# The second score product of 64-row heads over 128 rows, with zeros beside the keys' lower parts

## The chip, the cores and the metric

The kernel runs on one core of one Trainium2 chip. The metric is the device time of one execution in microseconds; smaller is better.

## What is computed

One batch of 512 tokens of width 1024 goes through two blocks. The first is a feed-forward layer, a mixer (retention and differential attention side by side), a cross-attention to a memory of 256 tokens and a second feed-forward layer. The second block is a neighbourhood attention, a gated embedding, a latent attention (MLA) and a second gated embedding. All is in float32. Three of the attentions have heads of 64 values; their scores are what the change is about:

```
retention       inner = einsum('bhnd,bhmd->bhnm', q, k) * decay          # 4 heads, d = 64
differential    s = einsum('bqhcd,bkhcd->bhcqk', q, k) * scale           # 4 heads x 2, d = 64
neighbourhood   s = einsum('bwhd,biwjhd->bhwij', q, k) * scale           # 16 heads, d = 64
```

The latent attention has heads of 96 values and is not touched; the cross-attention is not touched either.

## The kernel before

TensorE works on float32 operands that are split into an upper part (rounded to what TensorE takes) and a lower part (the rest). An ordinary product is three products, upper x upper, lower x upper and upper x lower (`mm3`, lines 265 to 267), accumulated in one PSUM tile. A split is a copy on ScalarE (upper part) and a subtraction on VectorE (lower part).

Weights come in pieces of 128 x 1024 through the SyncE queue, are split by ScalarE (L231) and VectorE (L232) and are held in three buffers. A projection tile is 8 steps of k with 3 products of 512 columns each.

**Scores of 64-row heads.** Two heads lie on top of each other in one 128-row tile. `stacked` (L462) makes the operands. For the operand that stands still in TensorE (`st`), one tile for each head holds the head's upper part in its own 64 rows and its lower part in the other 64. For the operand that moves (`mv`), one tile for each head holds the upper part twice (the second copy by a DMA, `move`, L1755), and a third tile, `x[2]`, holds the lower parts of both heads, each in its own 64 rows. `mm_stacked` (L490) then makes the scores with two products:

```
mm(out, st[hh][:, cs], mv[hh][:, cm], start=True, stop=False)      # L494: (upper; lower) x (upper; upper), 128 rows
mm(out, st[hh][r, cs], mv[2][r, cm], start=False, stop=True)       # L495: upper x lower, the head's 64 rows
```

It is called by `ret_s` (L800: 4 heads x 4 key tiles, 512, 384, 256 and 256 columns), by `dif_s` (L866: 4 heads x 4 query blocks, two calls behind each other in each, 256, 256, 384 and 512 columns) and by `s` of the neighbourhood attention (L1351: 16 heads x 4 query blocks, 256 columns): 16 + 32 + 64 = 112 pairs of products.

**Order.** TensorE and SyncE run in the order in which the program emits. The emission follows a clock of TensorE's work that the builder adds up (`pe`), and what the other engines do is put into a queue of events with delays. Between the scores, the transposes and the products with the values of an attention step, `fill` emits projection products ("filler"), in amounts given by the table `FILL`; the steps lie `LAG` apart (transposes two steps after the scores, products with values three or four). So while an attention waits for its softmax, TensorE has other work.

The set of operand tiles `y` (8 pairs `yh`, `yl` of 128 x 512) holds the feed-forward layer's hidden tiles, then the outputs of an attention's heads, and is read by the projection that follows. Head outputs are split into it at the end of a head (`ys`).

The row factors of a norm come by a chain (`rstd_chain`): TensorE transposes sums (L291), VectorE reduces (L304, L306), GpSimd takes a power (L311, tile `rs`), and TensorE transposes again (L317).

Of the kernel before, what the change touches and what calls it, by code (L numbers as in the profile page):

```python
# [11 lines left out]
F32R = mybir.dt.float32r  # L12
# [27 lines left out]
class Pr:  # L40
    """Whether the instructions that make something are emitted."""
# [6 lines left out]
class Act:  # L48
    """The two parts of an operand of a product."""
# [5 lines left out]
class Rows:  # L55
    """Factors of the rows of something: rs by partition, rb along the free axis."""
# [6 lines left out]
class Norm(Rows):  # L63
    """Operands x * gain, without the row factors, which come when all of x has been added."""
# [11 lines left out]
    def add(self, x, k, delay, later=0.0):  # L76
        """x, the k-th tile, is there delay us from now; its squares are not wanted until later us after that."""
# [28 lines left out]
class Builder:  # L106
    """Emits the program. Every engine runs its instructions as they are emitted; the emission follows a
    clock of the tensor engine, and what other engines do is emitted when its operands should be there."""
# [19 lines left out]
    # ------------------------------------------------------------- order of emission  # L128
# [3 lines left out]
    def ev(self, delay, fn, pr=None):  # L132
        """fn is emitted delay us from now."""
        pr = pr or Pr()
        self.seq += 1
        heapq.heappush(self.heap, (self.now() + delay, self.seq, fn, pr))
        return pr
# [12 lines left out]
    def when(self, pr, fn):  # L150
        """fn, which frees a product's place, is emitted as soon as pr is."""
        if pr.done:
            self.ev(0.1, fn)
        else:
            pr.then.append(fn)
            self.parked += 1
            self.parked_on = pr
# [20 lines left out]
    def fill(self, us):  # L178
        """Emits filler products worth us, as far as there are any."""
# [5 lines left out]
    # ------------------------------------------------------------- tiles  # L185
# [8 lines left out]
    def act(self, which, k):  # L194
        """The k-th tile pair of one of the two sets of operands."""
# [4 lines left out]
    # ------------------------------------------------------------- weights  # L200
# [17 lines left out]
    def halved(i, n):  # L218
        """The first pieces of all come in two halves, so that the arithmetic can begin."""
# [16 lines left out]
    def wget(self, pieces):  # L236
        """pieces: [(name, first row, columns)], 128 rows each, side by side."""
# [24 lines left out]
    # ------------------------------------------------------------- products  # L262
# [18 lines left out]
    # ------------------------------------------------------------- norms  # L281
    def rstd_chain(self, acc, nt, d, out, pr, slack, more=None):
        """From now on: sums over the partitions of acc [128, nt*128] give out.rs [128 tok, nt] and out.rb [128, nt*128]."""
# [51 lines left out]
    # ------------------------------------------------------------- parts that several phases have  # L335
    def gemm_list(self, items, acts, nk=KT, late=0):
        """items: [(pieces, evac(psum))], one product of 512 columns each. The first two take their last
        operands late."""
# [26 lines left out]
    def gate(self, cond):  # L365
        """Filler that has to wait for the attention to get on."""
# [8 lines left out]
    def proj(self, name, ys, xt, nxt, k0=0, nk=KT, scale=None, early=0, late=1):  # L375
        """x += y @ W (times scale); feeds the sums and operands of the next norm. The last early tiles have
        got the first half of it before."""
# [19 lines left out]
    def pairs(self, name, ms, acts, k0, nk, item):  # L397
        """Products of few k, two to a piece of weights."""
# [9 lines left out]
    def proj_early(self, name, ys, xt, early):  # L408
        """x += the first half of y @ W for the last early tiles."""
# [7 lines left out]
    def vproj(self, name, cols, acts, ntok, dst, nk=KT, w=None):  # L417
        """Rows of tokens of 256 columns: dst(i, psum) for every tile of tokens."""
# [22 lines left out]
    def split(self, hi, lo, src, delay=0.1, scale=None, pr=None, n=512):  # L441
        """hi and lo of src (times scale), which is there delay from now."""
# [19 lines left out]
    def stacked(self, mp, t, tag, moving, delay, pr):  # L462
        """Parts of t, two heads of 64 rows that are there delay from now, for products over 64 rows in two steps:
        upper and lower part on top of each other times the upper part twice, upper times lower part. Gives
        [first head, second head] or, of the operand that moves, [first head, second head, lower parts]."""
        nc = self.nc
        x = [mp.tile([P, 512], F32R, tag=f"{tag}{i}", name=self.nm(tag), bufs=2) for i in range(3 if moving else 2)]
# [9 lines left out]
        def second():  # L477
            a, b = (x[2][lo, :], x[2][hi, :]) if moving else (x[0][hi, :], x[1][lo, :])
# [10 lines left out]

    def mm_stacked(self, out, st, mv, hh, cs, cm):  # L490
        """out = product of columns cs of st and cm of mv over the rows of a head."""
        mm = self.nc.tensor.matmul
        r = slice(64 * hh, 64 * hh + 64)
        mm(out, st[hh][:, cs], mv[hh][:, cm], start=True, stop=False)  # L494
        mm(out, st[hh][r, cs], mv[2][r, cm], start=False, stop=True)  # L495
        self.pe(2 * out.shape[-1] / 2400)

    def softmax(self, sp, bias=None, to=None):
        """Rows of sp (psum [128 q, n]), plus bias if any, to probabilities in sbuf; returns (tile, Pr)."""
# [33 lines left out]
    def transposed(self, pt, hi, lo, n):  # L533
        """pt (psum) to hi and lo, as parts."""
        return self.split(hi, lo, pt, 0.1, n=n)

    def halves(self, t, hh, po, pr):
        """t[rows of head hh] = upper + lower half of po."""
# [13 lines left out]
    def gated(self, o, z, y, *prs):  # L552
        """y = o * z as parts, once prs are there."""
# [6 lines left out]
    def silu(self, z, ps, n, pr):  # L560
        """z = silu(ps times the row factors of n) from now on, as h + h tanh h with h half of the argument."""
# [13 lines left out]
    # ------------------------------------------------------------- phases  # L575
# [40 lines left out]
    def mix(self, n, xt, nxt):  # L616
        nc, tc = self.nc, self.tc
        with tc.tile_pool(name="mixp", bufs=1) as mp:
# [35 lines left out]
            for y in ys:  # L654
                y.pr = Pr()
# [1368 lines left out]
```

## Time and profile before

| | |
|---|---|
| median of 3 runs | 1880.83 us (1880.43 to 1881.2) |
| span of the profiled execution | 1879.1 us; its own time is not listed apart, and the median is 1.7 us above this span |
| TensorE busy (products) | 1846.8 us, 98% |
| TensorE weight loads | 1529.3 us, 81% |
| VectorE / ScalarE / GpSimd busy | 59% / 43% / 17% |
| mean DMA rate | 96 GB/s |
| retention | 397.7 to 489.9 us |
| differential attention | 489.9 to 586.5 us (its last scores), its tail to about 605 us |
| neighbourhood attention | 1190 to 1437 us (its last scores), its tail to about 1450 us |

Products are pipelined: the duration of one is longer than the distance to the next, and its end is modelled. What a product costs is read from start to start. Weight loads have rows of their own (PEld) and run beside the product before.

### The profile page before, as it was taken

What the parts mean: (1) busy time and instruction counts of PE and PEld (TensorE: products, weight loads), DVE (VectorE), ACT (ScalarE), POOL (GpSimd) and SP (SyncE); (2) the same over time, 40 slices, a digit from 0 to 9 for tenths busy, and PEclk for the clock granted to TensorE, in tenths of its full rate; (3) what the DMA queues carried; (4) which work ended last, traced back from release to release, by engine and by line L of the source; (5) the groups of instructions that cost most, each with busy time, mean ns of one, the idle gap of its engine ahead of it and who ended that gap; (6) DMA issues with size and microseconds to landing.
All of it is one profiled execution on the core that took longest, in us unless ns stands there. A gap on an engine that the chain in (4) does not pass through costs nothing.

```text
span 1879.1 us, 24338 instructions
## 1 busy us (share of the span) xinstructions
PE 1846.8 (98%) x9176; PEld 1529.3 (81%) x9176; DVE 1103.2 (59%) x1806; ACT 813.9 (43%) x1416; POOL 327.2 (17%) x317
## 2 busy tenths in 40 slices
PE   9999999999999999999999998999999999999997
PEld 7888888888876898888888886788888887888886
DVE  6434444556776755544344445666666667888646
ACT  5222222433554544432232234555554544666644
POOL 2000000310112211200000004322222221444322
PEclk9999999999999999999999999999999999999998
DMA  4222222422221332222323222323232223434222
GB/s 159 98 93 101 91 101 97 142 69 84 80 79 56 112 135 77 92 91 89 110 91 103 98 87 97 115 88 115 88 104 70 95 95 88 110 91 110 86 90 79
DMA packets 55556, 181.13 MB, mean 96 GB/s; under 512 B 7104, under 2 KB 9792, under 8 KB 55440
## 3 DMA queue, kind: packets, MB, share of 16 engines
q1 hardware_dynamic: 52480, 168.45, 27.3%
q0 software_dynamic: 2816, 11.08, 1.8%
q8 instruction: 73, 1.20, 0.3%
q14 instruction: 43, 0.35, 0.1%
q10 hardware_dynamic: 144, 0.05, 0.0%
HBM read 163.04 MB, written 2.10 MB: 88 GB/s over the span
## 4 chain that ended last, share of the span: by engine, by line
PE 92%; DVE 3%; ACT 2%; POOL 1%; issue 1%; DMA 1%; POOLq 0%; SPq 0%; DVEq 0%; ACTq 0%
PE mm L265 24%; PE mm L266 24%; PE mm L267 24%; PE mm L434 2%; PE mm L435 2%; PE mm L436 2%; PE sc L495 2%; PE av L1712 1%; PE tp L1690 1%; PE av L1394 1%; PE sc L494 1%; PE tp L1378 1%; PE sc L265 1%; PE sc L266 1%; PE sc L267 1%
## 5 line engine op out<-in xcount | busy, mean ns | idle before, releaser
L231 ACT ACTIVATE whi<-raw 128x1024 fp32r<-128x1024 f32 (+3 forms) x302 | 304.5, 1013 | 623.9 <-PE mm L266 429.5
L265 PE MATMUL mm<-xh,whi 128*128 128x512 f32 x1152 | 461.9, 401 | 3.5 <-ACT xh L450 3.5
L266 PE MATMUL mm<-xl,whi 128*128 128x512 f32 x1152 | 451.8, 392 | 5.7 <-DVE xl L457 5.6
L267 PE MATMUL mm<-xh,wlo 128*128 128x512 f32 x1152 | 451.3, 392 | 0.0
L232 DVE TENSOR_TENSOR wlo<-raw,whi 128x1024 fp32r<-128x1024 f32 (+3 forms) x302 | 363.7, 1207 | 64.5 <-ACT whi L231 61.1
L265 PE MATMUL mm<-yh,whi 128*128 128x512 f32 (+2 forms) x736 | 287.6, 391 | 2.3 <-ACT yh L448 2.3
L266 PE MATMUL mm<-yl,whi 128*128 128x512 f32 (+2 forms) x736 | 284.5, 387 | 0.5 <-DVE yl L455 0.5
L267 PE MATMUL mm<-yh,wlo 128*128 128x512 f32 (+2 forms) x736 | 284.2, 386 | 0.0
L265 PEld LDWEIGHTS mm<-xh,whi 128*128 128x128 f32 x1152 | 217.1, 188 | 55.5 <-ACT xh L450 5.2
L266 PEld LDWEIGHTS mm<-xl,whi 128*128 128x128 f32 x1152 | 217.5, 189 | 52.2 <-DVE xl L457 10.4
L267 PEld LDWEIGHTS mm<-xh,wlo 128*128 128x128 f32 x1152 | 217.1, 188 | 46.5 <-DVE wlo L232 0.3
L265 PEld LDWEIGHTS mm<-yh,whi 128*128 128x128 f32 (+1 forms) x736 | 138.1, 188 | 32.5 <-ACT yh L448 2.5
L267 PEld LDWEIGHTS mm<-yh,wlo 128*128 128x128 f32 (+1 forms) x736 | 138.2, 188 | 28.9
L266 PEld LDWEIGHTS mm<-yl,whi 128*128 128x128 f32 (+1 forms) x736 | 138.1, 188 | 28.3 <-DVE yl L455 1.1
L528 POOL TENSOR_TENSOR p<-p,st 128x512 f32<-128x512 f32 (+1 forms) x112 | 100.0, 895 | 249.5 <-DVE st L523 234.6
L99 POOL TENSOR_TENSOR acc<-acc,sq 128x512 f32<-128x512 f32 x54 | 92.7, 1718 | 166.9 <-ACT sq L95 166.5
L597 DVE TENSOR_TENSOR t<-mm,rb 128x512 f32<-128x512 f32 x44 | 30.4, 692 | 138.7 <-PE mm L267 138.7
L386 DVE SCALAR_TENSOR_TENSOR x<-mm,x 128x512 f32<-128x512 f32 x48 | 33.0, 691 | 119.9 <-PE mm L267 119.9
L588 DVE TENSOR_TENSOR t<-mm,rb 128x512 f32<-128x512 f32 x44 | 30.4, 692 | 94.2 <-PE mm L267 93.4
L434 PE MATMUL mm<-whi,xh 128*128 128x256 f32 x256 | 76.0, 297 | 0.0
L436 PE MATMUL mm<-whi,xl 128*128 128x256 f32 x256 | 72.4, 283 | 0.0
L435 PE MATMUL mm<-wlo,xh 128*128 128x256 f32 x256 | 72.4, 283 | 0.0
(315 smaller groups left out, 2807.2 us busy)
## 6 DMA issues: line engine op xcount, KB each, us to landing
raw<-in_wts SPq DMA_DIRECT2D x245, 512.0 KB, 3.5
raw<-in_wts SPq DMA_DIRECT2D x32, 448.0 KB, 3.3
bias<-in_nabias POOLq DMA_DIRECT2D x16, 384.0 KB, 3.4
kslot<-kt SPq DMA_DIRECT2D x16, 256.0 KB, 3.0
qs<-qt SPq DMA_DIRECT2D x16, 256.0 KB, 3.9
mv<-mv SPq DMA_DIRECT2D x28, 128.0 KB, 2.2
raw<-in_wts SPq DMA_DIRECT2D x12, 256.0 KB, 3.4
raw<-in_wts SPq DMA_DIRECT2D x8, 320.0 KB, 3.7
```

What stands on the lines that cost most here:

```text
L99: (nc.vector if k == KT - 1 else nc.gpsimd).tensor_tensor(self.acc, self.acc, t, OP.add)
L231: self.nc.scalar.activation(hi[:, c], raw[:, c], AF.Copy)
L232: pr = self.ev(0.3 + n / 1200, lambda c=c: self.nc.vector.tensor_tensor(lo[:, c], raw[:, c], b32(hi[:, c]), OP.subtract))
L265: mm(out, lh, rh, start=start, stop=False)
L266: mm(out, lh, rl, start=False, stop=False)
L267: mm(out, ll, rh, start=False, stop=stop)
L386: nc.vector.scalar_tensor_tensor(xt[m], ps, scale, xt[m], OP.mult, OP.add)
L434: mm(o, a.hi[:, t], w.hi[:, c], start=k == 0, stop=False)
L435: mm(o, a.hi[:, t], w.lo[:, c], start=False, stop=False)
L436: mm(o, a.lo[:, t], w.hi[:, c], start=False, stop=k == nk - 1)
L495: mm(out, st[hh][r, cs], mv[2][r, cm], start=False, stop=True)
L528: nc.gpsimd.tensor_tensor(p[:, :n], p[:, :n], st[:, 2:3].to_broadcast([P, n]), OP.mult)
```

## The change

The lower parts of the keys no longer share one tile. Each head gets a tile of its own for them, with the lower part in the head's own 64 rows and zeros in the other 64, and the second product runs over all 128 rows: the stationary tile's upper part meets the lower part, its lower part meets zeros. The zeros are written once at the start of the mixer and once at the start of the neighbourhood attention, into tiles 6 and 7 of the set `y`, which are free then; there are two pairs of such tiles, used in turn. The heads that write their outputs to tiles 6 and 7 take them when they are done. In the retention it is the queries that move, and the lower parts are theirs.

```diff
 def stacked(self, mp, t, tag, moving, delay, pr):
-    x = [mp.tile([P, 512], F32R, tag=f"{tag}{i}", name=self.nm(tag), bufs=2) for i in range(3 if moving else 2)]
+    x = [mp.tile([P, 512], F32R, tag=f"{tag}{i}", name=self.nm(tag), bufs=2) for i in range(2)]
+    if moving:
+        self.zi = 1 - self.zi
+        x.append(self.zl[self.zi])
...
     def second():
-        a, b = (x[2][lo, :], x[2][hi, :]) if moving else (x[0][hi, :], x[1][lo, :])
+        a, b = (x[2][0][lo, :], x[2][1][hi, :]) if moving else (x[0][hi, :], x[1][lo, :])
         nc.vector.tensor_tensor(a, t[lo, :], b32(x[0][lo, :]), OP.subtract)
         nc.vector.tensor_tensor(b, t[hi, :], b32(x[1][hi, :]), OP.subtract)
...
+def zeroed(self, tiles):
+    self.zi = 0
+    self.zl = [tiles[0:2], tiles[2:4]]
+    def zero():
+        for two in self.zl:
+            for c, t in enumerate(two):
+                self.nc.gpsimd.memset(b32(t[64 - 64 * c:128 - 64 * c, :]), 0.0)
+    self.zpr = self.ev(6.0, zero)
+
 def mm_stacked(self, out, st, mv, hh, cs, cm):
     mm = self.nc.tensor.matmul
-    r = slice(64 * hh, 64 * hh + 64)
+    self.need(self.zpr)
     mm(out, st[hh][:, cs], mv[hh][:, cm], start=True, stop=False)
-    mm(out, st[hh][r, cs], mv[2][r, cm], start=False, stop=True)
+    mm(out, st[hh][:, cs], mv[2][hh][:, cm], start=False, stop=True)
     self.pe(2 * out.shape[-1] / 2400)
...
 def mix(self, n, xt, nxt):
-    ys = [self.act("y", k) for k in range(KT)]
+    ys = [self.act("y", k) if k < 6 else Act(None, None) for k in range(KT)]
...
+    zs = [self.act("y", k) for k in (6, 7)]
...
     self.filler = prep()
+    self.zeroed([t for z in zs for t in (z.hi, z.lo)])
...
     # dif_av, done():
+    if h >= 2:
+        a = self.act("y", 4 + h)
+        ys[4 + h].hi, ys[4 + h].lo = a.hi, a.lo
     self.split(ys[4 + h].hi, ys[4 + h].lo, o, 0.75, pr=ys[4 + h].pr)
...
 def na(self, n, xt, nxt):
+    self.zeroed([t for z in [self.act("y", k) for k in (6, 7)] for t in (z.hi, z.lo)])
```

The order of instructions is the same before and after on TensorE, ScalarE and SyncE, but for the tile that the second product reads. TensorE, a score pair of the neighbourhood attention between a product with values (`av`) and filler (`mm`), before:

```order
L1394 MATMUL av_11360<-pt_9108,v_10446 128x256
L494 MATMUL sc_11369<-mv_11017,st_11072 128x256
L495 MATMUL sc_11369<-mv_11019,st_11072 128x256
L265 MATMUL mm_11315<-xh_9095,whi_11123 128x512
L266 MATMUL mm_11315<-xl_9096,whi_11123 128x512
```

and after the change:

```order
L1418 MATMUL av_11363<-pt_9110,v_10451 128x256
L510 MATMUL sc_11372<-mv_11021,st_11075 128x256
L511 MATMUL sc_11372<-yh_9115,st_11075 128x256
L265 MATMUL mm_11318<-xh_9097,whi_11126 128x512
L266 MATMUL mm_11318<-xl_9098,whi_11126 128x512
```

The second product of the pair now reads a `y` tile in place of the third `mv` tile; its neighbours are the same. (The list does not show that one has 64 rows and the other 128.)

GpSimd gets 8 memsets of 64 x 512. Four of them stand early in its queue, ahead of transfers and long idle time. The other four stand in two pairs, each between the last sum of squares of a norm (`acc`, L99) and the norm's power (`rs`, L311). The first of these places, at the end of the first feed-forward layer, before:

```order
L99 TENSOR_TENSOR acc_2348<-acc_2348,sq_2463 128x512
L99 TENSOR_TENSOR acc_2348<-acc_2348,sq_2499 128x512
L99 TENSOR_TENSOR acc_2348<-acc_2348,sq_2535 128x512
L311 TENSOR_TENSOR rs_2645<-rv_2639,small 128x4
L696 TENSOR_TENSOR t_2691<-t_2678,rcs 128x512
```

and after:

```order
L99 TENSOR_TENSOR acc_2348<-acc_2348,sq_2463 128x512
L99 TENSOR_TENSOR acc_2348<-acc_2348,sq_2499 128x512
L99 TENSOR_TENSOR acc_2348<-acc_2348,sq_2535 128x512
L502 MEMSET yl_2589 64x512
L502 MEMSET yh_2588 64x512
L311 TENSOR_TENSOR rs_2649<-rv_2639,small 128x4
L714 TENSOR_TENSOR t_2695<-t_2682,rcs 128x512
```

The two memsets wait for the last products that read tile 6 of `y`, and the power `rs` is queued behind them. The second such place is the same, at the end of the second feed-forward layer.

VectorE has one instruction elsewhere: at the end of the neighbourhood attention the lower part of head output 6 (`yl<-o,yh`) stands five places later. Its tile held zeros beside a lower part until the last score was made, so it waits for that product; the instruction right behind it (L527, the row maxima of that last score) waits for the same product.

## Rows read from the trace of the kernel before

**Rows 1.** The page's busy times and its chain of work that ended last, shares by engine.

```profile
PE 1846.8 (98%) x9176; PEld 1529.3 (81%) x9176; DVE 1103.2 (59%) x1806; ACT 813.9 (43%) x1416; POOL 327.2 (17%) x317
PE 92%; DVE 3%; ACT 2%; POOL 1%; issue 1%; DMA 1%; POOLq 0%; SPq 0%; DVEq 0%; ACTq 0%
```

**Rows 2.** Busy time of each engine in the stretches of the retention, the differential and the neighbourhood attention: length, PE, PEld, DVE, ACT, POOL busy (instructions), granted TensorE clock as a share of full speed, DMA share, GB/s.

```profile
397.70:489.90 92.20, 92.14 (x500) 75.65 (x499) 61.09 (x94) 37.17 (x61) 8.99 (x8) 1.00 0.24 81
489.90:586.50 96.60, 96.35 (x487) 75.11 (x486) 71.06 (x187) 50.24 (x112) 20.87 (x22) 1.00 0.22 73
1190.00:1437.00 247.00, 247.00 (x1368) 203.70 (x1367) 161.41 (x382) 135.71 (x295) 59.74 (x84) 1.00 0.29 98
```

**Rows 3.** The two products of a score pair over the whole program: minimum, median and maximum duration in ns, first and last start, forms.

```profile
L494 PE MATMUL sc<-mv,st x112: 276/282/503, 398.0 to 1436.2; 128*128 128x256 f32 x88, 128*128 128x512 f32 x12, 128*128 128x384 f32 x12
L495 PE MATMUL sc<-mv,st x112: 378/381/500, 398.3 to 1436.5; 64*128 64x256 f32 x88, 64*128 64x512 f32 x12, 64*128 64x384 f32 x12
```

**Rows 4.** TensorE in order of time around one score pair of the neighbourhood attention: start us, duration us, engine, line, operation, stationary rows * columns, moving operand.

```profile
1201.74 0.40 PE L267 MATMUL mm<-xh,wlo 128*128 128x512 f32 x1
1201.98 0.28 PE L494 MATMUL sc<-mv,st 128*128 128x256 f32 x1
1202.19 0.38 PE L495 MATMUL sc<-mv,st 64*128 64x256 f32 x1
1202.50 0.50 PE L265 MATMUL mm<-xh,whi 128*128 128x512 f32 x1
1202.83 0.40 PE L266 MATMUL mm<-xl,whi 128*128 128x512 f32 x1
```

**Rows 5.** TensorE at products over 128 rows behind each other, of 384 columns and of 512 and 256, in the retention.

```profile
483.27 0.34 PE L265 MATMUL av<-ah,vh 128*128 128x384 f32 x1
483.45 0.34 PE L266 MATMUL av<-al,vh 128*128 128x384 f32 x1
...
486.31 0.39 PE L267 MATMUL mm<-xh,wlo 128*128 128x512 f32 x1
486.54 0.28 PE L265 MATMUL av<-ah,vh 128*128 128x256 f32 x1
486.66 0.28 PE L266 MATMUL av<-al,vh 128*128 128x256 f32 x1
```

**Rows 6.** The weight loads around the score pair of rows 4, same columns.

```profile
1201.75 0.19 PEld L494 LDWEIGHTS sc<-mv,st 128*128 128x128 f32 x1
1202.19 0.18 PEld L495 LDWEIGHTS sc<-mv,st 64*128 64x128 f32 x1 [0.25 <-issue]
1202.49 0.19 PEld L265 LDWEIGHTS mm<-xh,whi 128*128 128x128 f32 x1
```

**Rows 7.** TensorE at a score pair of the retention with 512 columns, first row the first product of the pair, last row the second filler product behind it.

```profile
397.96 0.40 PE L494 MATMUL sc<-mv,st 128*128 128x512 f32 x1
...
399.04 0.40 PE L266 MATMUL mm<-xl,whi 128*128 128x512 f32 x1
```

**Rows 8.** TensorE at two score pairs behind each other in the differential attention, 384 columns: the first product of the first pair, and the second filler product behind the second pair.

```profile
501.72 0.34 PE L494 MATMUL sc<-mv,st 128*128 128x384 f32 x1
...
503.43 0.39 PE L266 MATMUL mm<-xl,whi 128*128 128x512 f32 x1
```

**Rows 9.** TensorE in the latent attention, a change from 128 to 96 rows.

```profile
1694.28 0.28 PE L1712 MATMUL av<-ptl,s 128*128 128x256 f32 x1
1694.39 0.40 PE L265 MATMUL sc<-kslot,qs 96*128 96x512 f32 x1
1694.62 0.40 PE L266 MATMUL sc<-kslot,qs 96*128 96x512 f32 x1
```

**Rows 10.** Neighbourhood attention: the row maxima of a score (VectorE), and the first product of the score two steps later, which writes the same PSUM buffer (TensorE).

```profile
1339.74 0.42 DVE L511 CUSTOM_DVE_ANT_0 pm<-sc,bias 128x256 f32<-128x256 f32 x1 [1.39 <-PE sc L495]
...
1342.85 0.28 PE L494 MATMUL sc<-mv,st 128*128 128x256 f32 x1
```

**Rows 11.** Differential attention: the power of a head's norm (GpSimd), and on TensorE two score pairs and the transposes that wait for the power.

```profile
570.36 1.01 POOL L311 TENSOR_TENSOR rs<-rv,small 128x4 f32<-128x4 f32 x1 [1.07 <-DVE rv L306]
...
569.42 0.36 PE L494 MATMUL sc<-mv,st 128*128 128x256 f32 x1
570.03 0.39 PE L494 MATMUL sc<-mv,st 128*128 128x256 f32 x1
572.14 0.38 PE L317 MATMUL tp<-ident,rs 128*128 128x128 f32 x2
```

**Rows 12.** The lower part of a head output on VectorE in the neighbourhood attention (busy us, mean ns of one), and TensorE's one wait at the end of the mixer.

```profile
L455 DVE TENSOR_TENSOR yl<-o,yh 128x512 fp32r<-128x512 f32 x7 | 5.3, 751 | 4.9 <-ACT yh L448 4.9
604.62 0.50 PE L265 MATMUL mm<-yh,whi 128*128 128x512 f32 x1 [2.26 <-ACT yh L448]
```

**Rows 13.** The two places of the new memsets on GpSimd: the power `rs` at each, the last TensorE product ahead of it that reads a tile of `y`, and the group of 128 x 512 sums on GpSimd (busy us, mean ns of one).

```profile
371.52 0.39 PE L267 MATMUL mm<-yh,wlo 128*128 128x512 f32 x1
1151.82 0.39 PE L267 MATMUL mm<-yh,wlo 128*128 128x512 f32 x1
378.12 1.04 POOL L311 TENSOR_TENSOR rs<-rv,small 128x4 f32<-128x4 f32 x1 [7.03 <-DVE rv L306]
1157.06 1.03 POOL L311 TENSOR_TENSOR rs<-rv,small 128x4 f32<-128x4 f32 x1 [6.34 <-DVE rv L306]
L99 POOL TENSOR_TENSOR acc<-acc,sq 128x512 f32<-128x512 f32 x54 | 92.7, 1718 | 166.9 <-ACT sq L95 166.5
```

## The prediction

> **What bounds the kernel now.** First the page: TensorE has products running in 98% of the span and makes up 92% of the chain that ended last [rows 1]. Then the busy times of the three stretches that the change touches: in the retention and the differential attention TensorE is idle for 0.06 and 0.25 us, in 247 us of the neighbourhood attention for none, and its clock is granted in full in all three [rows 2]. The other engines have room: VectorE, the next, is busy 66%, 74% and 65%. So a microsecond that TensorE no longer needs there should come off the time, unless another engine turns out late.
>
> But a busy TensorE is not one at its peak, since the durations overlap. The two products of a score pair write the same number of columns, and yet the one over 64 rows takes 381 ns and the one over 128 rows 282 ns at the median [rows 3]. What a pair costs is seen in the starts [rows 4]. The first product of the pair starts at 1201.98, the second, over 64 rows, 0.21 later, the next 0.31 later, and the one after that 0.33 later. Elsewhere, with 128 rows throughout, what follows a product of 512 columns starts 0.23 us behind it, 384 columns take 0.18 and 256 take 0.12 [rows 5]. The loads show why [rows 6]: the load of the first product runs beside the product before (1201.75 against a product start at 1201.74), but the load for 64 rows begins only at 1202.19, together with its own product, after 0.25 us in which the loader stood still, and the load that follows it again only at 1202.49. The loader cannot run ahead into or out of the 64-row product; the pipe of TensorE runs empty twice at each pair.
>
> **The change part by part.**
>
> *The pair itself.* Removed: 112 products over 64 rows. Added: 112 over 128 rows with the same columns. I take it that a 128-row product among 128-row products has the ordinary distance. From the start of the pair to the start of the second product behind it:
>
> - Neighbourhood attention, 256 columns: 1202.83 - 1201.98 = 0.85 us. Ordinary: 0.12 + 0.12 + 0.23 = 0.47. Saved 0.38. 64 pairs: 24.3 us.
> - Retention, 512 columns: 399.04 - 397.96 = 1.08 [rows 7], ordinary 3 x 0.23 = 0.69, saved 0.39; 16 pairs, the narrower ones taken alike: 6.2 us.
> - Differential attention, two pairs behind each other, 384 columns: 503.43 - 501.72 = 1.71 [rows 8], ordinary 4 x 0.18 + 0.23 = 0.95, saved 0.76 for two pairs; 16 such: 12.2 us.
>
> Together 42.7 us, 0.38 a pair. Bounds: if only the step into the 64-row product went (0.21 to 0.12) and what lies behind it stayed, 0.09 a pair, 10 us; reading errors of 0.02 us a pair upwards, 45 us. I take 42.7, since a product of 96 rows, which also fills less than the array, follows a 128-row product after 0.11 us and is followed after 0.23 [rows 9]: a product that leaves rows out does not by itself empty the pipe, one over 64 does. The Trainium skill, "TensorEngine Tiling (Array Packing)", Tiling Modes, Key Properties, says that a change of the tiling mode, not merely of the tile, drains TensorE, and it lists 64 rows as a mode and 96 not; the trace agrees, with two empty stretches a pair, and by that rule the whole 0.38 goes.
>
> *Freed time given back.* Steps get 0.38 us shorter (0.76 in the differential attention), while the chains of the other engines keep their length. In the neighbourhood attention the shortest reserve of a score's PSUM buffer is 1342.85 - (1339.74 + 0.42) = 2.69 us [rows 10]; two pairs within it take 0.77 away. Nothing is lost there. In the differential attention a head's norm has a power that ends at 571.37 and transposes that wait for it at 572.14: 0.77 us reserve, and the two pairs at 569.42 and 570.03 lie close to it [rows 11]. They are worth 0.76, so this wait comes to about zero, and a few others like it may cost some tenths. The wait of 2.26 us at the end of the mixer [rows 12] stays: its chain begins after the last scores, and the pairs before shift it as a whole. Given back: 0 to 3 us, I take 0.7.
>
> *The memsets.* Four of the eight stand ahead of transfers, where GpSimd has long been idle, and cost nothing. The other four stand in two places ahead of a norm's power. No memset of this size is in the trace; above, I take the sums of 128 x 512 on GpSimd, 1.72 us each [rows 13], below, nothing; nearest is the sum, for its engine and its 512 columns, and it is dear for a memset of half the rows. They may begin when the last product that reads the tile is done (371.52 + 0.39 = 371.9 and 1151.82 + 0.39 = 1152.2 [rows 13]) and end by 375.3 and 1155.6 at the latest; the powers start at 378.1 and 1157.1. They are hidden with 2.8 and 1.5 us to spare. If that cover were gone, each microsecond past it would stand on TensorE, which waits for the power's transposes.
>
> *Moved on VectorE, and the rest.* One subtraction of 0.75 us [rows 12] now stands ahead of the last score's row maxima and waits for the product that these wait for too; it delays them by 0.75 us, against a reserve of 2.69: nothing. The subtractions write two tiles in place of one, equally many and equally large; no transfer is added or moved on any queue.
>
> Sum: 42.7 - 0.7 = 42 us. The profiled execution has a span of 1879.1 us, which would become 1837; the median of the runs lies 1.7 us above that span, so 1880.8 becomes **1838.8 us**, 2.2% less.
>
> **The rivals.**
>
> *The time comes back as waits.* The fillers were laid out for steps of the old length, and VectorE's load in the differential attention rises from 74% to 71 / 84 = 84%. Against it: the reserves above, and that TensorE idles there for 0.3 us in all now [rows 2]. If a third of the gain came back, mostly in the differential attention and the norms: 14 us, 1853 us.
>
> *The gap belongs to the place, not to the 64 rows,* and the change does not do what it says. If the second load stood still because it reads the tile that the first has just loaded, or if a load ran ahead only into rows that are not in use, full rows would not help and the distances of 0.21, 0.31 and 0.33 would stay: 1880 us, no change; with only the step into the second product gone, 10 us, 1871 us. "TensorE: Matmul & The Clock Gate" of the Trainium skill, Part 3, What overlaps and what doesn't, says that weight loads overlap running products only when their row groups differ; by it full rows never overlap. The trace differs: the load at 1201.75 covers all 128 rows and starts beside a product over all 128 rows [rows 4, 6].
>
> *Slower, by the memsets.* GpSimd's power of a norm is queued behind two memsets at two places, and TensorE behind the power. Past the reserves of 2.8 and 1.5 us, each place costs its excess. To turn a gain of 42 us into a loss of over 3.8 us, the four memsets would need 46 + 4.3 + the 6.9 already allowed = 57 us, 14 us each, eight times the nearest row. If the pair's gain failed as well, 3.8 us of loss would need (3.8 + 4.3 + 6.9) / 4 = 3.8 us each, 1885 us. That is the point from which it decides.
>
> **How the numbers follow.** A measurement of this kernel can tell about 0.2%, 3.8 us, from no change. The forecast, 1833 to 1845: 0.79. The time given back, 1845 to 1862: 0.11. Only the step into the product, about 1871: 0.05. No change: 0.03, of it 0.01 for loads that run ahead only into unused rows. Slower: 0.02. The range has the first case whole and about half of the second: 1833 to 1851 us, some 0.85. Faster by over 0.2%: 0.95; within it 0.03; slower 0.02.
>
> **What would show it.** Right: the second product of a pair (L511 in the changed kernel) at about 282 ns, as the first; starts 0.12 us apart in a pair of 256 columns and 0.23 behind; loads of second products that begin beside the first; the neighbourhood attention shorter by about 24 us, the differential by 12 and the retention by 6, and everything outside unchanged. Given back: new waits of TensorE for `rs`, for row maxima or for split weights. Memsets: waits of L317 for `rs` at 379 and near 1140 us. The forecast is wrong if the loads of second products still begin with their own product, or if the three stretches shrink by less than 35 us together.

## The result and the profile after

The changed kernel takes 1840.38 us at the median (1839.84 to 1841.4, 4 runs) against 1880.98 us (1880.43 to 1881.2, 4 runs) for the kernel before: ratio 0.9785, 95% interval 0.9771 to 0.9799. The forecast was 1838.8 us in a range of 1833 to 1851. The span of the profiled execution falls from 1879.1 to 1838.2 us.

Where rows of the kernel after follow, they answer to rows shown of before, named by their groups. First the page, busy times and chain, beside [rows 1]:

```profile
PE 1803.2 (98%) x9176; PEld 1520.4 (83%) x9176; DVE 1098.7 (60%) x1806; ACT 810.9 (44%) x1416; POOL 330.1 (18%) x325
PE 91%; DVE 3%; ACT 2%; POOL 2%; issue 1%; DMA 0%; SPq 0%; POOLq 0%; DVEq 0%; ACTq 0%
```

TensorE still bounds the kernel. The number of its products is the same, and their busy time is 43.6 us less; the weight loads are busy 8.9 us less only. Most of what went from the span, 32.0 of 40.9 us, is time in which the loader stood still (349.8 us before, 317.8 after: span less busy time).

The two products of a pair over the whole program, beside [rows 3] (minimum, median, maximum in ns, first and last start; the second product reads `yh` for one head of a tile and `yl` for the other; the row shown is that of `yh`):

```profile
L510 PE MATMUL sc<-mv,st x112: 277/283/500, 398.4 to 1395.5; 128*128 128x256 f32 x88, 128*128 128x512 f32 x12, 128*128 128x384 f32 x12
L511 PE MATMUL sc<-yh,st x56: 274/283/400, 398.7 to 1386.6; 128*128 128x256 f32 x44, 128*128 128x512 f32 x6, 128*128 128x384 f32 x6
```

The second product has come from 381 to 283 ns, the first's own value. One pair of the neighbourhood attention in order of time, beside [rows 4], and its loads, beside [rows 6]:

```profile
1185.23 0.28 PE L510 MATMUL sc<-mv,st 128*128 128x256 f32 x1
1185.34 0.28 PE L511 MATMUL sc<-yh,st 128*128 128x256 f32 x1
1185.46 0.40 PE L265 MATMUL mm<-xh,whi 128*128 128x512 f32 x1
1185.70 0.40 PE L266 MATMUL mm<-xl,whi 128*128 128x512 f32 x1
...
1185.01 0.19 PEld L510 LDWEIGHTS sc<-mv,st 128*128 128x128 f32 x1
1185.23 0.19 PEld L511 LDWEIGHTS sc<-yh,st 128*128 128x128 f32 x1
1185.35 0.19 PEld L265 LDWEIGHTS mm<-xh,whi 128*128 128x128 f32 x1
```

The starts lie 0.11, 0.12 and 0.24 apart, 0.47 in all where it was 0.85. Each load begins with the product before it: the load of L511 at 1185.23, where L510 starts, and that of L265 at 1185.35, where L511 has just started. The 0.25 us of stillness ahead of the second load is gone.

The three stretches, cut at the same instructions as in [rows 2], with its columns:

```profile
398.16:484.04 85.88, 85.84 (x500) 75.26 (x499) 60.86 (x94) 37.25 (x61) 8.99 (x8) 1.00 0.27 87
484.04:570.10 86.06, 84.44 (x488) 73.30 (x488) 69.25 (x186) 48.58 (x112) 19.22 (x22) 1.00 0.26 79
1173.65:1395.90 222.25, 222.25 (x1368) 197.13 (x1367) 158.42 (x379) 133.38 (x293) 59.00 (x83) 1.00 0.33 109
```

The retention is 6.3 us shorter, the differential attention 10.5, the neighbourhood attention 24.75. Since TensorE's order did not change, every instruction of one trace can be set against the same one of the other: their difference is +0.46 us up to the retention (one wait at the start of the program came out longer), -5.9 behind it, -16.4 behind the differential attention, the same -16.4 until the neighbourhood attention begins, and -41.1 from its end to the end of the program. Outside the three stretches nothing moved.

Of the three stretches only the differential attention has TensorE idle more than before: 1.62 us where it was 0.25 (and two waits in its tail, behind the last scores, are 0.24 us longer each). The largest piece is one wait, at the transposes that [rows 11] show with a reserve of 0.77 us. In the trace after, TensorE reaches the transposes that feed this norm (L291) at 553.08; then VectorE, GpSimd and TensorE:

```profile
553.08 0.60 PE L291 MATMUL tp<-ident,t 128*128 128x128 f32 x4
554.18 0.68 DVE L304 TENSOR_REDUCE rv<-tp 128x4 f32<-128x512 f32 x1
555.51 0.75 DVE L929 SCALAR_TENSOR_TENSOR p<-p,dst,p 128x512 f32<-128x512 f32 x1 [0.65 <-POOL p L925]
556.17 0.16 DVE L306 TENSOR_SCALAR rv<-rv 128x4 f32<-128x4 f32 x1
556.48 1.01 POOL L311 TENSOR_TENSOR rs<-rv,small 128x4 f32<-128x4 f32 x1 [1.01 <-DVE rv L306]
557.54 0.65 PE L317 MATMUL tp<-ident,rs 128*128 128x128 f32 x4 [1.09 <-POOL rs L311]
```

and the same place before, TensorE's L291 and VectorE (L910 is what is now L929):

```profile
568.15 0.60 PE L291 MATMUL tp<-ident,t 128*128 128x128 f32 x4
568.79 0.69 DVE L304 TENSOR_REDUCE rv<-tp 128x4 f32<-128x512 f32 x1 [0.70 <-PE tp L291]
569.39 0.74 DVE L910 SCALAR_TENSOR_TENSOR p<-p,dst,p 128x512 f32<-128x512 f32 x1
570.05 0.16 DVE L306 TENSOR_SCALAR rv<-rv 128x4 f32<-128x4 f32 x1
```

From L291 to L306 it took 1.90 us before and takes 3.09 now. On VectorE a step of the softmax (L929) that waits for GpSimd stands ahead of L306, which starts only when that step is nearly done (556.17). TensorE comes to L291 15.07 us earlier than before, but that step comes only 13.88 us earlier, so the norm's chain grew by 1.19 us besides losing 0.76 us of cover. 1.19 + 0.76 - 0.77 = 1.18, and the wait is 1.09.

The memsets, in the first of the two places where something could have waited for them (GpSimd), beside [rows 13], and the transposes behind:

```profile
372.20 0.52 POOL L502 MEMSET yl<- 64x512 f32 x1 [0.66 <-PE mm L266]
372.78 0.52 POOL L502 MEMSET yh<- 64x512 f32 x1
378.64 1.04 POOL L311 TENSOR_TENSOR rs<-rv,small 128x4 f32<-128x4 f32 x1 [5.35 <-DVE rv L306]
...
380.18 0.60 PE L317 MATMUL tp<-ident,rs 128*128 128x128 f32 x4
```

A memset takes 0.52 us, where the nearest row gave 1.72. GpSimd then waits 5.35 us for its input, and L317 waits for nothing. The second place is the same (1135.69 to 1136.78, power at 1140.77 after 3.99 us of waiting; L317 waits 0.08 us there, where it was 0.01).

### The profile page after: what moved, and what is told of

It reads as the page before. It is cut to its first block, busy times and chain, and to the rows that moved or that the text cites. A ratio compares the mean times of both kernels' runs of the same rounds, so it can differ in the third digit from the quotient of the medians.

```text
span 1838.2 us, 24354 instructions
## 1 busy us (share of the span) xinstructions
PE 1803.2 (98%) x9176; PEld 1520.4 (83%) x9176; DVE 1098.7 (60%) x1806; ACT 810.9 (44%) x1416; POOL 330.1 (18%) x325
## 4 chain that ended last, share of the span: by engine, by line
PE 91%; DVE 3%; ACT 2%; POOL 2%; issue 1%; DMA 0%; SPq 0%; POOLq 0%; DVEq 0%; ACTq 0%
PE mm L266 24%; PE mm L265 24%; PE mm L267 24%; PE mm L434 2%; PE mm L435 2%; PE mm L436 2%; PE av L1736 1%; PE tp L1714 1%; PE av L1418 1%; PE tp L1402 1%; PE sc L265 1%; PE sc L266 1%; PE sc L267 1%; POOL acc L99 1%; PE sc L510 1%
## 5 line engine op out<-in xcount | busy, mean ns | idle before, releaser
L265 PE MATMUL mm<-xh,whi 128*128 128x512 f32 x1152 | 455.5, 395 | 3.9 <-ACT xh L450 3.9
L265 PE MATMUL mm<-yh,whi 128*128 128x512 f32 (+2 forms) x736 | 286.5, 389 | 2.3 <-ACT yh L448 2.3
L265 PEld LDWEIGHTS mm<-xh,whi 128*128 128x128 f32 x1152 | 217.4, 189 | 48.0 <-ACT xh L450 5.7
L265 PEld LDWEIGHTS mm<-yh,whi 128*128 128x128 f32 (+1 forms) x736 | 138.0, 188 | 30.8 <-ACT yh L448 2.5
L99 POOL TENSOR_TENSOR acc<-acc,sq 128x512 f32<-128x512 f32 x54 | 92.4, 1712 | 167.9 <-ACT sq L95 167.5
```

Source lines behind the costliest of these rows:

```text
L99: (nc.vector if k == KT - 1 else nc.gpsimd).tensor_tensor(self.acc, self.acc, t, OP.add)
L265: mm(out, lh, rh, start=start, stop=False)
```

## Experiments

The theory: an isolated product over 64 rows among products over 128 makes TensorE's loader stand still on entering and on leaving, 0.38 us in all, wherever it stands. The rivals: that the gap belongs to the place of the second product (the same stationary tile as the product before it, the accumulation); that any product with fewer than 128 rows has it; that memsets are dearer than they look; that the differential attention gives more back than its waits show.

**Grouping in place of padding** (on the kernel before). The order of a double pair of the differential attention becomes first, first, second, second, still with 64 rows in the second products:

```diff
+    w = max(nn, 256)
+    sps = [self.ps("sc") for _ in range(2)]
...
     for c in range(2):
-        sp = self.ps("sc")
-        w = max(nn, 256)
-        self.mm_stacked(sp[:, :w], qs, ks, c, t, slice(0, w))
+        mm(sps[c][:, :w], qs[c][:, t], ks[c][:, 0:w], start=True, stop=False)
+    for c in range(2):
+        r = slice(64 * c, 64 * c + 64)
+        mm(sps[c][:, :w], qs[c][r, t], ks[2][r, 0:w], start=False, stop=True)
...
```

> The kernel before, with the four products of a step of the differential attention in another order: both first products (128 rows), then both second products (64 rows each, the upper and the lower half of the rows). Theory (the pipe runs empty once on the way into and once on the way out of a stretch of 64-row products, 0.38 us a stretch): 16 stretches in place of 32, 16 x 0.38 = 6.1 us less, 1874.8 us; if the two 64-row products also run side by side, up to 16 x 0.12 us more, 1873. Rival 'place' (the second load stands still because it reads the stationary tile that the first one has just loaded): the first load of the other head now lies between, so both gaps would go, 32 x 0.2 to 32 x 0.38 = 6 to 12 us. Rival 'each product that leaves rows out pays': no change, 1880.8.

Measured: 1873.41 us (1872.75 to 1874.6, 5 runs) against 1880.76, ratio 0.9961 (0.9947 to 0.9974): 7.35 us gained. TensorE and its loads at one such group of 384 columns (x2: two instructions behind each other):

```profile
501.12 0.52 PE L882 MATMUL sc<-mv,st 128*128 128x384 f32 x2
501.57 0.44 PE L885 MATMUL sc<-mv,st 64*128 64x384 f32 x2
501.94 0.50 PE L265 MATMUL mm<-xh,whi 128*128 128x512 f32 x1
502.28 0.39 PE L266 MATMUL mm<-xl,whi 128*128 128x512 f32 x1
...
500.89 0.42 PEld L882 LDWEIGHTS sc<-mv,st 128*128 128x128 f32 x2
501.57 0.19 PEld L885 LDWEIGHTS sc<-mv,st 64*128 64x128 f32 x2 [0.26 <-issue]
501.94 0.19 PEld L265 LDWEIGHTS mm<-xh,whi 128*128 128x128 f32 x1 [0.18 <-issue]
```

From the first start to 502.28 it is 1.16 us, where [rows 8] have 1.71 and products over 128 rows throughout would have 0.95. The stillness of the loader stands once a group (0.26 us on the way in, 0.18 on the way out), not once a pair. The load that stands still follows the load of the other head's tile, so its cause is not that it reads the tile just loaded. The two loads over 64 rows take 0.19 us together, as one alone does, and the two products 0.44 us together, no longer than one of them: they start 3 ns apart, at every width. Upper and lower half of the rows work beside each other.

So the 0.55 us that a group saves has two parts: one way in and out less (0.38), and a second product that costs no distance of its own (0.18 at 384 columns). By the median starts of the three widths (256, 384, 512 columns) it is 8 x 0.50 + 4 x 0.56 + 4 x 0.60 = 8.6 us. Of these the trace gives back about 1.6 us in the same attention, 0.54 and 0.45 of it at the transposes that wait for `rs`; 7.35 was measured. The time alone does not tell the theory from the rival of the place, which had 6 to 12 us; the loads do.

**Both products over 64 rows** (on the kernel before, neighbourhood attention only; the lower parts of the queries are left out of the scores there, since the first product runs over the head's upper part alone):

```diff
-    mm(out, st[hh][:, cs], mv[hh][:, cm], start=True, stop=False)
+    q = r if self.half else slice(0, 128)
+    mm(out, st[hh][q, cs], mv[hh][q, cm], start=True, stop=False)
...
 def na(self, n, xt, nxt):
+    self.half = True
```

> The kernel before, with the first product of a score pair of the neighbourhood attention over the head's 64 rows too; it leaves out the product of the lower parts of the queries with the upper parts of the keys. Theory (each stretch of 64-row products pays once, on the way in and on the way out): a stretch is now two products long, no gap between them, the same price as before: 1880.8 us, within 2. Rival 'each product that leaves rows out pays' (0.38 each): 64 x 0.38 = 24 us more, 1905. Rival 'place' (the second load waits for the first one's tile): the gap of 0.21 between the two stays and nothing is added, 1880.8 too, but the starts then still lie 0.2 apart inside the pair, where the theory has 0.12.

Measured: 1880.53 us (1879.71 to 1881.55, 10 runs), ratio 0.9999 (0.999 to 1.0008). The pair and its two loads:

```profile
1201.59 0.40 PE L267 MATMUL mm<-xh,wlo 128*128 128x512 f32 x1
1201.91 0.38 PE L495 MATMUL sc<-mv,st 64*128 64x256 f32 x1
1202.14 0.28 PE L496 MATMUL sc<-mv,st 64*128 64x256 f32 x1
1202.35 0.50 PE L265 MATMUL mm<-xh,whi 128*128 128x512 f32 x1
1202.68 0.40 PE L266 MATMUL mm<-xl,whi 128*128 128x512 f32 x1
...
1201.91 0.18 PEld L495 LDWEIGHTS sc<-mv,st 64*128 64x128 f32 x1 [0.36 <-issue]
1202.02 0.19 PEld L496 LDWEIGHTS sc<-mv,st 64*128 64x128 f32 x1
```

From the product ahead of the pair to the second behind it: 1.09 us, and 1.09 before [rows 4]. One 64-row product or two, the price is one. Theory and rival of the place both had this time, and inside the pair the starts lie 0.23 apart (0.22 at the median of the 64 pairs): that is the rival's sign, not the theory's 0.12. The loads speak against the rival. The one that stands still is now the first product's (0.36 us), and the second product's load starts at 1202.02, ahead of its own product, though it reads the same tile as the first.

The starts suggest how the price is made up. What they have above the ordinary distance is 0.09, 0.19 and 0.10 around a single 64-row product [rows 4], and 0.09, 0.11, 0.09 and 0.10 here. So it looks as if the first product behind a change of rows comes 0.09 us late and the next another 0.10, on the way in as on the way out, and the 0.23 inside the pair would be the second of these. No run tests this by itself.

**64 rows elsewhere** (on the changed kernel; in the fourth k step of the gate and up products of the first and second feed-forward layer, 88 products, half the rows of the product with the weights' lower part are left out):

```diff
+    if self.cut and k == 3:
...
+        mm(out, w.hi[:, c], a.hi, start=False, stop=False)
+        mm(out, w.hi[:, c], a.lo, start=False, stop=False)
+        mm(out, w.lo[0:64, c], a.hi[0:64, :], start=False, stop=False)
...
```

> The changed kernel, with one product of the feed-forward layers' gate and up projections (the third of the fourth k, 88 in all, 512 columns) over 64 rows; the other 64 rows of that step are left out. No score, no stationary tile that is read twice running. Theory: 88 x 0.39 = 34 us more, 1875 us, with loads of those products that begin with their own product. Rival 'place' (the gap belongs to the score pair): no change, 1840.4.

Measured: 1874.35 us (1873.96 to 1875.61, 5 runs; ratio to the kernel before 0.9968, 0.9955 to 0.998), 34.0 us over the changed kernel: 0.386 us each. The group of these loads and products, with the loader's idle time ahead of them:

```profile
L278 PE MATMUL mm<-xh,wlo x88: 493/498/502, 12.2 to 1129.8; 64*128 64x512 f32 x88
its engine sat idle before it (us, times) until:
  issue: 31.3, 88
```

All 88 have it, 0.36 us of idle loader apiece. Here the stationary operand is not that of the product before, the accumulation goes on, and neighbours are ordinary weights: the gap belongs to the 64 rows.

**96 rows** (on the changed kernel). For the first head of each tile the second product leaves out the last 32 rows, which hold zeros:

```diff
-    mm(out, st[hh][:, cs], mv[2][hh][:, cm], start=False, stop=True)
+    r = slice(0, 96) if hh == 0 else slice(0, 128)
+    mm(out, st[hh][r, cs], mv[2][hh][r, cm], start=False, stop=True)
```

> The changed kernel, with the second product of the upper head of each pair of heads (56 of 112) over 96 rows, 32 rows of zeros, in place of 128. Theory in the form that 96 rows run in the same way of working as 128: no change, 1840.4. Rival 'each product that leaves rows out pays': 56 x 0.38 = 21 us more, 1862.

Measured: 1840.11 us (1839.62 to 1841.63, 4 runs; ratio 0.9785, 0.9772 to 0.9799), as the changed kernel. Products over 96 rows have 284 ns at the median, those over 128 rows 283. So leaving out 32 rows costs nothing, and leaving out 64 does; other counts were not tried.

**Second product left out** (on the changed kernel; upper x lower is missing in all 112 pairs):

```diff
-    mm(out, st[hh][:, cs], mv[hh][:, cm], start=True, stop=False)
-    mm(out, st[hh][:, cs], mv[2][hh][:, cm], start=False, stop=True)
+    mm(out, st[hh][:, cs], mv[hh][:, cm], start=True, stop=True)
```

> The changed kernel without the second product of a score pair (the upper parts of the queries times the lower parts of the keys are left out). Theory (TensorE still sets the pace of the score stages, and a second product costs its ordinary distance): 88 x 0.12 + 12 x 0.18 + 12 x 0.23 = 15.5 us less than 1840.4, 1825 us; a little is given back in the differential attention, so 1825 to 1827. Rival 'the other engines have become the bound of those stages': clearly less than 15 us, 1832 or more.

Measured: 1830.83 us (1829.56 to 1831.01, 4 runs; ratio 0.9731, 0.9718 to 0.9745), 9.6 us under the changed kernel where the starts promised 15.5, between theory and rival. By the same instruction in both traces: the neighbourhood attention gave 7.5 of 7.7, the retention 2.4 of 2.6, and the differential attention with its tail lost 0.4 where 5.2 had been expected; 0.9 was lost in the latent attention, where a wait for a transfer came up, and 0.45 came from the program's start. TensorE's waits in the differential attention:

```profile
529.64 0.65 PE L317 MATMUL tp<-ident,rs 128*128 128x128 f32 x4 [0.77 <-POOL rs L311]
553.24 1.12 PE L317 MATMUL tp<-ident,rs 128*128 128x128 f32 x4 [2.90 <-POOL rs L311]
572.86 0.63 PE L941 MATMUL tp<-ident,p 128*128 128x128 f32 x4 [1.35 <-DVE p L928]
```

The wait of 1.09 us has become 2.90 at the same transposes, and behind it TensorE ran at the lower clock for a while: granted 0.60 over the next 3.8 us (the column behind the engines' busy times), a mean of the level of 1.2 GHz and that of 2.4, while it stayed full behind the 1.09 us.

```profile
553.20:557.00 3.80, 3.76 (x15) 3.19 (x16) 2.32 (x6) 0.62 (x2) 0.40 (x1) 0.60 0.38 124
557.00:560.00 3.00, 3.00 (x19) 2.61 (x18) 2.43 (x8) 1.59 (x5) 0.00 (x0) 1.00 0.05 21
```

So the differential attention has no reserve left after the change: what TensorE saves there now comes back whole. The theory of the gap is not touched by it; the estimate was too large because it took the stretch for bound by TensorE.

**Ten memsets for each one** (on the changed kernel):

```diff
-    for c, t in enumerate(two):
+    for c, t in [x for x in enumerate(two) for _ in range(10)]:
```

> The changed kernel with each of the 8 memsets ten times. One takes 0.52 us in the changed kernel's trace and they follow at 0.58. Theory (they are hidden up to a point and then stand on TensorE, one for one): ahead of the first norm's power 20 of them, 11.5 us from 372.2, end at 383.7; the power began at 378.6, and its transposes had 0.5 us more: 4.6 us later. Ahead of the second power 12 of the 20 stand in the queue, 6.9 us from 1135.7, end at 1142.6; the power began at 1140.8: 1.8 us later, and 8 more memsets lie ahead of the sums of the next norm, 0 to 4.6 us. In all 6.4 to 11 us more than 1840.4: 1847 to 1851. Rival 'memsets on GpSimd stay hidden behind the products': no change.

Measured: 1847.69 us (1847.13 to 1847.83, 4 runs; ratio 0.9822, 0.9808 to 0.9835), 7.3 us more. The transposes behind the two places:

```profile
385.21 1.11 PE L317 MATMUL tp<-ident,rs 128*128 128x128 f32 x4 [4.47 <-POOL rs L311]
1150.32 0.65 PE L317 MATMUL tp<-ident,rs 128*128 128x128 f32 x4 [1.91 <-POOL rs L311]
```

Now they wait, 4.47 and 1.91 us, which shifts these two instructions by 4.63 and 1.84 us against the changed kernel's trace, as forecast. Behind the first wait another 1.4 us go, for the granted clock is 0.62 over the 4 us that follow, in part at the level of 1.2 GHz; behind the second, of 1.91 us, it stays full:

```profile
385.00:389.00 4.00, 3.79 (x13) 3.24 (x14) 0.00 (x0) 0.60 (x1) 0.15 (x1) 0.62 0.00 0
...
1150.00:1154.00 4.00, 3.68 (x18) 3.13 (x19) 2.88 (x3) 2.61 (x5) 3.67 (x8) 1.00 0.37 131
```

Behind the second place TensorE catches up 0.4 us at waits that it has there anyway. With 0.4 us of a longer start the span is 7.8 us longer, the median 7.3. The other two places lose nothing. The rival's mechanism is real and its path is as described (memset, power, transposes, TensorE); with one memset of 0.52 us in place of ten the power still waits for its input, and nothing is lost.

**More time for two norms** (on the changed kernel; the slack of the differential attention's norms shifts L317 behind more filler):

```diff
-    head_norm(PO.pop(h), done, SLACK["dif"])
+    head_norm(PO.pop(h), done, (0.48, (1.6, 2.2, 0.94, 0.94)[h]))
```

> The changed kernel, with the transposes that wait for a head norm's power in the differential attention emitted 0.7 us (first head) and 1.3 us (second head) later, so that more filler stands ahead of them. Theory (the gain lost in the differential attention is TensorE's waits of 0.5 and 1.1 us for these powers): 1.6 us less, 1838.8 us, and no wait for the power left there. Rival (the filler that fills the wait is missing elsewhere, or the outputs of the heads come late): no change, 1840.4.

Measured: 1841.96 us (1841.55 to 1843.52, 5 runs; ratio 0.9793, 0.978 to 0.9807). The forecast of 1838.8 us failed: the time is 1.6 us above the changed kernel's. The waits for `rs` in this stretch fell from 0.53 and 1.09 us to 0.23 us in all, and a wait at one of the last head's steps has taken their place:

```profile
576.27 1.09 PE L942 MATMUL tp<-ident,p 128*128 128x128 f32 x4 [2.99 <-DVE p L929]
...
576.20:580.00 3.80, 3.58 (x14) 3.03 (x15) 1.44 (x2) 1.53 (x3) 0.10 (x1) 0.50 0.00 0
```

Its 2.99 us, and the clock at 0.50 (1.2 GHz) in the 3.8 us behind it, cost more than the waits that went.

**More time for one norm** (as the last, for the second head alone):

```diff
-    head_norm(PO.pop(h), done, SLACK["dif"])
+    head_norm(PO.pop(h), done, (0.48, (0.94, 1.6, 0.94, 0.94)[h]))
```

> From the changed kernel: the norm of the second head of the differential attention alone gets more time (second delay 1.6 in place of 0.94), so that its transposes L317 stand behind one more group of three filler products of 512 columns (0.69 us by the starts); nothing else on TensorE moves, so the transposes and values of the later steps keep their places. Theory (the wait of 1.09 us for rs is the one loss that the shorter steps made in this head, and filler ahead of it covers it): the wait falls to about 0.4 us, TensorE is 0.6 to 0.7 us earlier from there on, and the time is 1839.7 us, which the trace can show and the times hardly. Rival (as with more time for two heads: the filler that is used here is missing a few steps later, and a wait for split weights p takes its place): 1840.4 us or more, with a new wait of L942.

Measured: 1841.26 us (1840.45 to 1841.87, 5 runs; ratio 0.9791, 0.9777 to 0.9804), not to be told from the changed kernel. TensorE's two waits, and VectorE's instruction ahead of the second:

```profile
557.60 0.65 PE L317 MATMUL tp<-ident,rs 128*128 128x128 f32 x4 [0.42 <-POOL rs L311]
574.30 0.55 PE L942 MATMUL tp<-ident,p 128*128 128x128 f32 x3 [2.02 <-DVE rv L304]
...
569.60 1.38 DVE L929 SCALAR_TENSOR_TENSOR p<-p,dst,p 128x384 f32<-128x384 f32 x1 [1.03 <-POOL p L925]
```

The first wait fell from 1.09 to 0.42, as the theory said, and TensorE ran 0.65 us earlier for the 16 us behind it; then its wait at the last steps of the last head grew from 0.80 to 2.02 us and took it all back. That place is paced by VectorE. The rival had the end right, a wait of L942, but not its cause: here no filler is missing, TensorE comes earlier and VectorE 0.55 later. So what was given back in this attention was not had by giving one or two of its norms more time; other places for the filler were not tried. No kernel here that computes everything is clearly faster than the changed one.

## Why the prediction was right

**The pair itself.** 42.7 us were forecast: 24.3, 6.2 and 12.2. The neighbourhood attention gave 24.75 and the retention 6.3. The differential attention gave 10.5 net; with 1.25, 0.27, 0.24 and 0.31 us, which TensorE lost at four waits there and in its tail, it is 12.6. So each term of the sum held to half a microsecond (43.6 us in all), and the extrapolation it rested on (a 128-row product behind a 128-row product has the ordinary distance) is shown by the starts of the pair. That a product pays nothing for leaving rows out as such, argued from the latent attention's 96 rows, is shown by the experiment with 96 rows; that the price is on the step into 64 rows and out of it, by the products elsewhere at 0.386 us. The rule of the Trainium skill on changes of the tiling mode ("TensorEngine Tiling (Array Packing)", Tiling Modes, Key Properties) agrees with three of the runs on rows (grouping, elsewhere, 96) and does not tell of the 0.23 us inside the pair of the fourth; what such a change costs here, 0.38 to 0.39 us there and back for one product, is the runs' number. That TensorE's pipe runs empty at it, as the prediction puts it, the traces don't show directly, since ends of products are modelled; they show the loader standing still and the later starts.

**Freed time given back.** 0.7 us were taken out of 0 to 3; 2.1 were given back in the differential attention and its tail. This term was sized too small. The prediction held the other engines' chains at their length and only took TensorE's two pairs from the reserve; but the chain of the norm runs through VectorE's queue, in which an instruction of the softmax stands ahead, and it grew by 1.19 us when TensorE came earlier. Its place, the transposes of [rows 11], was named.

**The memsets.** Hidden, as forecast, with 5.35 and 3.99 us of idle time ahead of the power instead of 2.8 and 1.5: they take 0.52 us, less than a third of the row that was taken as nearest.

**The rest.** The subtraction moved on VectorE costs nothing: the neighbourhood attention has no idle TensorE and gave all its gain. The wait of [rows 12] stayed at 2.26 us. The forecast lies 1.6 us under the result, with errors of both signs in it. The pairs gave 0.9 more than forecast, 1.4 more came back (2.1 against 0.7), and the wait at the start of the program is 0.5 longer: the span is 1.1 us above the forecast one (1838.2 against 1837.1). The other 0.5 is that the median lies 2.2 us above the profiled span, where 1.7 was taken. That the forecast came so close is in part this cancelling.

**The rivals.** *The time comes back as waits*: in kind yes, in size no, 2.1 us of 14; the run without the second product shows how near the limit was, since the next 5 us in the differential attention all came back. *The gap belongs to the place*: refuted by the starts and loads after the change, and by 64 rows elsewhere; grouping and both products over 64 rows speak against it by their loads, not by their times. *Slower, by the memsets*: the path exists, and ten-fold memsets cost 7.3 us.

## What to carry to other kernels

Read TensorE by the distances of starts and by the loader's idle time, not by its busy share: 98% busy hid 43 us. A lone product over 64 rows among products over 128 is worth filling with zeros when the zeros can be written once and beside other work; where they can't, put the 64-row products of both halves behind each other, where they share one way in and out and run side by side. Before counting a gain in a stretch as whole, follow the shortest reserve through every engine's queue that the chain passes, for what stands ahead there may be late by its own clock.

## What the runs showed of the hardware

- Rows: 96 of 128 cost no more than 128 (284 and 283 ns); 64 of 128 cost 0.38 to 0.39 us for the way in and out, though the product has fewer rows.
- Two loads of 64 rows into opposite halves took 0.19 us together, and their two products of 384 columns 0.44 us together, started 3 ns apart (grouped run). Among 128-row products, loads run beside products over the same rows (load of L511 and product L510, both at 1185.23).
- TensorE's granted clock was at the level of 1.2 GHz for some or all of the 3.8 to 4 us behind waits of 2.90, 2.99 and 4.47 us (means 0.60, 0.50 and 0.62) and stayed full behind waits of 1.09, 1.91 and 2.02 us. The wait of 2.26 us at the end of the mixer went both ways: 0.68 over the 3.8 us behind it in the changed kernel, 1.00 behind the same wait in the run with both products over 64 rows. A wait that grows can so cost over a microsecond more than its own length (1.4 us behind the one of 4.47).
- GpSimd writes zeros into 64 x 512 float32 in 0.52 us; a sum of 128 x 512 takes 1.72.
- In the last run L929 on VectorE took 1.38 us, where the same 128 x 384 took 0.62 in the changed kernel. A GpSimd instruction of 1.04 us (L807) had started 0.07 us ahead of it; in the changed kernel L929 had started first, and L807 took 1.31 us. Whichever came second was the longer one. The Trainium skill, "SBUF — State Buffer", Who interferes with whom, says that a VectorE instruction with two inputs in SBUF contends with a reading GpSimd instruction for a shared port, and that the order of issue decides who blocks; the two traces agree, in this one pair of instructions.
